# A four-layer decoder trunk: the first norm's squares and row dealt out over later blocks, a load moved to ACT's queue, and halved matmuls in the odd mixer

## The chip, the core and the metric

The kernel runs on one core of a Trainium2 chip. The metric is the time of one execution on the device in microseconds; of several executions the median is given.

## What is computed

The reference is a decoder trunk for 256 positions of 1024 channels: two layers, each with a feed-forward block (FFN), a mixer and a second FFN, all added to the residual with an RMS norm ahead of each. The even layer's mixer is latent attention beside a pooling mixer, the odd one's a gated spatial mixer. Cut to what matters here:

```python
def _rmsnorm(x, g):
    xf = x.astype(jnp.float32)
    y = xf * lax.rsqrt(jnp.mean(xf * xf, axis=-1, keepdims=True) + EPS)
    return (y * g.astype(jnp.float32)).astype(x.dtype)

def _swiglu(x, w_gate, w_up, w_down):
    return (jax.nn.silu(x @ w_gate) * (x @ w_up)) @ w_down
...
        h = h + 0.5 * _swiglu(_rmsnorm(h, ffn_norm[layer, 0]), ffn_w_gate[layer, 0],
                              ffn_w_up[layer, 0], ffn_w_down[layer, 0])
```

All of it is in float32. FFN width is 2816.

## The kernel before

Activations lie transposed, channels on partitions: hT holds eight k tiles of 128 x 256. The order of the work on each engine is the order in which the program is written; nothing is rescheduled.

**Weights** come in chunks of 512 KB, in one list for the whole program (chunks 0 to 43 are the first FFN's gate and up weights, four chunks to a block of 256 hidden channels, so block b uses chunks 4b to 4b+3; a chunk holds two k tiles). A chunk is loaded by SP into one of five `raw` buffers, cast by ACT to a high part `whi` (L170), and DVE takes the difference as the low part `wlo` (L178); I call that DVE step the chunk's split. There are six pairs of high and low. `next_chunk` (L197) hands out a chunk and before that emits the casts and splits of chunks up to three ahead (`LOOK`), fewer for the first chunks (the `min(look, max(1, i - 2))`). The first four chunks, the head, are split in halves or quarters (L182, L183).

**A matmul** of full accuracy is a pair, `mm2` (L215): `wlo` times the high part of x, 256 columns (L217), and `whi` times both parts of x, 512 columns (L218). The two halves of the bank are added when it is evacuated: ACT copies one half (`a`, L325), DVE adds the other (`gu`, L327).

**The FFN** (L355) works through 11 blocks. `gate_up(b)` runs 64 pairs into four PSUM banks, from the pools `acc` and `rot` in turn; `hooks` are called ahead of a given chunk of the block. Then comes the evacuation, then `epilogue(b)`: DVE multiplies by the norm's row, ACT takes silu, DVE multiplies twice, ACT casts, DVE takes the difference (L382 to L388).

**The norm** is applied late. x is only scaled by the gain (`norm_hi` on ACT, `norm_lo` on DVE). The squares are taken by ACT (L274) and summed by POOL (L279). `norm_sum` (L282) sums over partitions on TensorE (L285), DVE adds epsilon (`me`, L288), POOL takes the power (L251) and builds four diagonal matrices (L298), two high and two low. `norm_row` (L301) turns them into a row in PSUM by four matmuls of 128 columns (L305, L307), which ACT copies to `rb` (L310) and DVE halves to `rbh` (L314). In each FFN the sum runs ahead of block 1's first chunk (the bank is one that block 0's evacuation frees) and the row and block 0's epilogue ahead of its third.

**The head of the program** (from L1052): 18 warm-up matmuls on zeros, then loads on SP in turn: par_x0 (gains and the first k tile), the chunk's piece, the next k tile, and so on, then the constants `cst` (identity and masks). For each k tile ACT casts x and the weights and DVE takes the differences; the squares of k tile k-2 follow behind.

**The odd mixer's output** (L1021 on) multiplies `zz`, the gated product, by the output weights, two k tiles to a chunk; `mix_block(3)`, `gate(3)` and `gate_lo(3)` (L1004), which make the last two k tiles of zz, stand behind the first chunk.

## Time and profile before

| | us |
|---|---|
| median of 3 runs | 902.7 (899.63 to 903.33) |
| the profiled execution | 899.92 |
| its span on the core | 898.1 |
| TensorE matmuls busy | 887.7 |
| DVE busy | 651.0 |
| ACT busy | 498.5 |
| POOL busy | 99.7 |

The durations below come from the one profiled execution; its time is the span and 1.8 us around it. A busy TensorE is not one at its peak: matmuls overlap, so what counts is when each starts. Engines are written PE (matmul), PEld (its weight loads), DVE, ACT, POOL and SP; L218 is line 218.

### The profile page before, as it was taken

How to read it: one execution, taken by the hardware profiler on the slowest of the kernel's cores; microseconds unless marked ns; L12 is line 12 of the kernel's file. 1: busy time of each engine (PE TensorE's matmuls, PEld its weight loads, DVE VectorE, ACT ScalarE, POOL GpSimd, SP SyncE). 2: the span in 40 equal slices, each digit the busy share in tenths (PEclk: the TensorE clock that was granted, in tenths of full speed). 3: DMA queues.
4: the chain of work that ended last, by engine and by line, in shares of the span. 5: the costliest groups of instructions: out<-in, count | busy, mean ns of one | idle time of the engine just before them, and what ended most of it. 6: DMA issues, size and time to landing. Idle time of an engine off the chain costs nothing.

```text
span 898.1 us, 13674 instructions
## 1 busy us (share of the span) xinstructions
PE 887.7 (99%) x5204; PEld 783.2 (87%) x5204; DVE 651.0 (72%) x989; ACT 498.5 (56%) x790; POOL 99.7 (11%) x130
## 2 busy tenths in 40 slices
PE   8999999999999999999999999999999999999998
PEld 6888888899898888888888888888888888888887
DVE  7787778667877877785558777756658878777652
ACT  7555554547675655554456555544545666555430
POOL 4200000117524000000130000000120220000000
PEclk9999999999999999999999999999999999999999
DMA  8575556634344555557544555576435556555750
GB/s 291 187 248 195 193 191 194 218 116 161 110 150 141 180 191 196 185 189 241 202 157 149 188 188 188 188 261 190 167 128 168 167 185 202 194 191 189 257 165 24
DMA packets 60306, 164.45 MB, mean 183 GB/s; under 512 B 5457, under 2 KB 7761, under 8 KB 60241
## 3 DMA queue, kind: packets, MB, share of 16 engines
q1 hardware_dynamic: 60240, 163.58, 54.3%
q8 instruction: 41, 0.67, 0.3%
q14 instruction: 25, 0.20, 0.1%
HBM read 162.51 MB, written 1.05 MB: 182 GB/s over the span
## 4 chain that ended last, share of the span: by engine, by line
PE 90%; DVE 5%; POOL 2%; issue 1%; ACT 1%; DMA 1%; SPq 0%; DVEq 0%; ACTq 0%; POOLq 0%
PE acc L218 27%; PE rot L218 27%; PE acc L217 14%; PE rot L217 14%; PE rot L211 1%; PE rot L213 1%; PE rot L212 1%; DVE wlo L178 1%; POOL diag L298 1%; PE acc L212 1%; PE acc L211 1%; PE acc L213 1%; DMA raw<-w_gu 1%; DVE sA L611 0%; DVE z L994 0%
## 5 line engine op out<-in xcount | busy, mean ns | idle before, releaser
L178 DVE TENSOR_TENSOR wlo<-raw,whi 128x1024 fp32r<-128x1024 f32 (+2 forms) x298 | 352.9, 1229 | 71.4 <-ACT whi L170 71.3
L170 ACT CAST whi<-raw 128x1024 fp32r<-128x1024 f32 (+2 forms) x303 | 301.5, 1044 | 101.2 <-PE acc L218 40.5
L218 PE MATMUL acc<-x,whi 128*128 128x512 f32 x768 | 268.2, 392 | 0.0
L218 PE MATMUL rot<-x,whi 128*128 128x512 f32 x704 | 245.6, 392 | 0.0
L217 PE MATMUL acc<-x,wlo 128*128 128x256 f32 x768 | 216.6, 282 | 2.0 <-DVE wlo L183 1.9
L217 PE MATMUL rot<-x,wlo 128*128 128x256 f32 x704 | 197.5, 280 | 0.0
L218 PEld LDWEIGHTS acc<-x,whi 128*128 128x128 f32 x768 | 143.8, 187 | 31.1
L218 PEld LDWEIGHTS rot<-x,whi 128*128 128x128 f32 x704 | 131.7, 187 | 29.0
L217 PEld LDWEIGHTS acc<-x,wlo 128*128 128x128 f32 x768 | 145.4, 189 | 3.7 <-DVE wlo L183 3.2
L217 PEld LDWEIGHTS rot<-x,wlo 128*128 128x128 f32 x704 | 133.1, 189 | 0.0
L218 PE MATMUL rot<-pp,whi 128*128 128x512 f32 x352 | 122.2, 391 | 0.0
L218 PE MATMUL acc<-pp,whi 128*128 128x512 f32 x352 | 122.2, 391 | 0.0
L217 PE MATMUL rot<-pp,wlo 128*128 128x256 f32 x352 | 98.6, 280 | 0.0
L217 PE MATMUL acc<-pp,wlo 128*128 128x256 f32 x352 | 98.6, 280 | 0.0
L218 PEld LDWEIGHTS rot<-pp,whi 128*128 128x128 f32 x352 | 65.8, 187 | 14.4
L218 PEld LDWEIGHTS acc<-pp,whi 128*128 128x128 f32 x352 | 65.8, 187 | 14.4
L217 PEld LDWEIGHTS rot<-pp,wlo 128*128 128x128 f32 x352 | 66.5, 189 | 0.0
L217 PEld LDWEIGHTS acc<-pp,wlo 128*128 128x128 f32 x352 | 66.5, 189 | 0.0
L325 ACT COPY a<-rot 128x256 f32<-128x256 f32 x88 | 29.7, 374 | 52.1 <-PE rot L218 52.1
L325 ACT COPY a<-acc 128x256 f32<-128x256 f32 x88 | 29.7, 374 | 51.2 <-PE acc L218 51.1
L279 POOL TENSOR_TENSOR sqsum<-sq,sq 128x256 f32<-128x256 f32 x6 | 6.0, 1007 | 453.0 <-ACT sq L274 453.0
L383 ACT ACTIVATE gu<-gu 128x512 f32<-128x512 f32 x44 | 27.8, 633 | 50.7 <-DVE gu L382 50.6
(247 smaller groups left out, 937.2 us busy)
## 6 DMA issues: line engine op xcount, KB each, us to landing
raw<-w_gu SPq DMA_DIRECT2D x172, 512.0 KB, 4.7
raw<-w_down SPq DMA_DIRECT2D x88, 512.0 KB, 4.7
raw<-ew_out SPq DMA_DIRECT2D x8, 512.0 KB, 3.6
raw<-ow_v SPq DMA_DIRECT2D x8, 512.0 KB, 3.6
raw<-ow_u SPq DMA_DIRECT2D x8, 512.0 KB, 5.0
raw<-ow_out SPq DMA_DIRECT2D x8, 512.0 KB, 3.7
raw<-ew_p SPq DMA_DIRECT2D x4, 512.0 KB, 4.2
raw<-w_gu SPq DMA_DIRECT2D x7, 256.0 KB, 4.6
```

The lines of the kernel that those rows point to most:

```text
L170: nc.scalar.copy(hi[:, :n], r[:, :n])
L178: eng.tensor_sub(lo[:, :n], r[:, :n], hi[:, :n].bitcast(F32))
L211: nc.tensor.matmul(out, wl, xh, start=start, stop=False, skip_group_check=True)
L212: nc.tensor.matmul(out, wh, xl, start=False, stop=False, skip_group_check=True)
L213: nc.tensor.matmul(out, wh, xh, start=False, stop=stop, skip_group_check=True)
L217: nc.tensor.matmul(bank[:, 0:T], wl, x[:, 1, :], start=start, stop=False, skip_group_check=True)
L218: nc.tensor.matmul(bank, wh, x.rearrange("p s t -> p (s t)"), start=False, stop=stop, skip_group_check=True)
L279: nc.gpsimd.tensor_add(t, s.sum, sq)
L298: nc.gpsimd.tensor_scalar(s.dg[:, i, tb * P : (tb + 1) * P], ident, part[:, tb : tb + 1], None, op0=ALU.mult)
L325: nc.scalar.copy(tmp[:, i, :], bank[:, 0:T])
L383: nc.scalar.activation(t, t, AF.Silu)
```

## The change

- In the head: par_x0 is issued from ACT's queue; the first k tile's cast goes from ACT to DVE; a 19th warm-up matmul; no squares between the casts. `next_chunk` looks three chunks ahead from the start.
- In the first FFN: the squares are taken ahead of block 0's third chunk (k tiles 0 to 3) and fourth (4 to 7), and added by DVE in place of POOL. The constants are loaded ahead of block 0's second chunk, behind the loads of five more chunks. The sum runs ahead of block 1's third chunk. The row runs in two halves, ahead of block 2's second and third chunk, in a bank of its own; block 0's epilogue stands behind the second half, block 1's ahead of block 2's fourth chunk.
- In the other three FFNs the sum stays, the row's first half stays ahead of block 1's third chunk, and its second half and block 0's epilogue go ahead of the fourth.
- In the odd mixer: for the k tile behind `mix_block(3)`, the low-part matmuls of the first two output tiles run in two halves of 128 columns, ahead of both high-part ones.

```diff
-WARM = 18
-SQ_LAG = 2
+WARM = 19
...
-        advance(i + 1 + min(look, max(1, i - 2)), cap)
+        advance(i + 1 + look, cap)
...
-    def norm_sq(s, k):
+    def norm_sq(s, k, eng=nc.gpsimd):
...
-            nc.gpsimd.tensor_add(t, s.sum, sq)
+            eng.tensor_add(t, s.sum, sq)
...
-    def norm_row(s, half=False):
+    def norm_row(s, half=False, bank=None, parts=range(TB)):
+        s.bank = s.bank if bank is None else bank
         bc = s.bank[:, T : 2 * T]
-        for tb in range(TB):
+        for tb in parts:
...
+        if TB - 1 not in parts:
+            return
...
-            gu0 = evacuate(gate_up(0))
-            bank = sets[0]()
+            held = {}
+
+            def late(b):
+                epilogue(b, held.pop(b))
+
+            def row():
+                norm_row(s, bank=sets[1]() if first else None, parts=(0,))
 
             def mid():
-                norm_row(s, half=True)
-                epilogue(0, gu0)
-
-            for b in range(1, NB):
-                gb = gate_up(b, {0: lambda: norm_sum(s, bank), 2: mid} if b == 1 else {})
-                epilogue(b, evacuate(gb))
+                norm_row(s, half=True, parts=(1,))
+                late(0)
+
+            def squares(ks):
+                for k in ks:
+                    norm_sq(s, k, nc.vector)
+
+            if first:
+                hooks = {0: {1: lambda: nc.sync.dma_start(cst_sb, cst), 2: lambda: squares(range(4)),
+                             3: lambda: squares(range(4, KD))},
+                         1: {2: lambda: norm_sum(s, sets[0]())}, 2: {1: row, 2: mid, 3: lambda: late(1)}}
+            else:
+                hooks = {1: {0: lambda: norm_sum(s, sets[0]()), 2: row, 3: mid}}
+            for b in range(NB):
+                held[b] = evacuate(gate_up(b, hooks.get(b, {})))
+                if b > (1 if first else 0):
+                    late(b)
...
+                    n = 2 if j == 1 and k % 2 == 0 else 0
+                    for m in range(n):
+                        ms = slice(m * P, (m + 1) * P)
+                        for tb in range(TB):
+                            ts = slice(tb * P, (tb + 1) * P)
+                            nc.tensor.matmul(banks[m][:, ts], w[1][:, 0, ms], zz[:, k, 1, ts], start=False,
+                                             stop=False, skip_group_check=True)
...
+    nc.scalar.dma_start(par_h[:, 0 : NPAR + T], par_x0)
     preload(AF.Silu)
...
-            if k == 0:
-                nc.sync.dma_start(par_h[:, 0 : NPAR + T], par_x0)
-            else:
+            if k > 0:
                 nc.sync.dma_start(hT[:, k, :], xT[k - 1])
...
-    nc.sync.dma_start(cst_sb, cst)
...
-            norm_hi(s, k)
+            if k == 0:
+                nc.vector.tensor_scalar(s.xh[:, k, :], hT[:, k, :], pcol(s.gname, s.goff), None,
+                                        op0=ALU.mult)
+            else:
+                norm_hi(s, k)
             norm_lo(s, k)
         split(*parts[c], cs, nc.vector)
-        if k not in seen and k >= SQ_LAG:
-            norm_sq(s, k - SQ_LAG)
         seen.add(k)
-    for k in range(KD - SQ_LAG, KD):
-        norm_sq(s, k)
```

How the rows move is shown at three places. First ACT, behind the head, before: the last two casts of the head's casts, the last squares, the casts of chunks 4 and 5 (`raw_219`, `raw_221`), then block 0's evacuation.

```order
L182 CAST whi_145<-raw_133 128x512
L274 ACTIVATE sq_199<-par_h 128x256
L274 ACTIVATE sq_203<-par_h 128x256
L274 ACTIVATE sq_207<-par_h 128x256
L170 CAST whi_277<-raw_219 128x1024
L170 CAST whi_280<-raw_221 128x1024
L325 COPY a_303<-acc_215 128x256
```

The same place in the change; chunks 4 to 7 are `raw_189`, `raw_191`, `raw_193` and `raw_195`.

```order
L181 CAST whi_145<-raw_134 128x512
L169 CAST whi_216<-raw_189 128x1024
L169 CAST whi_219<-raw_191 128x1024
L273 ACTIVATE sq_241<-par_h 128x256
L273 ACTIVATE sq_243<-par_h 128x256
L273 ACTIVATE sq_247<-par_h 128x256
L273 ACTIVATE sq_251<-par_h 128x256
L169 CAST whi_255<-raw_193 128x1024
...
L169 CAST whi_293<-raw_195 128x1024
L327 COPY a_316<-acc_185 128x256
```

Eight squares and the casts of chunks 6 and 7 now stand ahead of block 0's evacuation, and four of the squares ahead of chunk 6's cast.

Second DVE, from `rbh` on in the first FFN, before: block 0's epilogue, the splits of chunks 9 and 10 (`raw_284`, `raw_336`), then block 1's evacuation, all in block 1.

```order
L314 TENSOR_SCALAR rbh_394<-acc_312 128x256
L382 TENSOR_TENSOR gu_302<-gu_302,rb_392 128x512
L384 TENSOR_TENSOR gu_302<-gu_302,rbh_394 128x512
L385 TENSOR_TENSOR gu_302<-gu_302 128x512
L388 TENSOR_TENSOR pp_214<-gu_302,pp_214 128x2x256
L178 TENSOR_TENSOR wlo_367<-raw_284,whi_366 128x1024
L178 TENSOR_TENSOR wlo_403<-raw_336,whi_402 128x1024
L327 TENSOR_TENSOR gu_446<-rot_313,a_447 128x256
```

And in the change, from `rbh` on, in block 2; chunks 13 and 14 are `raw_355` and `raw_393`, and the last row is the first of block 2's evacuation, behind which block 2's epilogue and only then the split of chunk 15 stand.

```order
L316 TENSOR_SCALAR rbh_498<-rot_469 128x256
L384 TENSOR_TENSOR gu_315<-gu_315,rb_496 128x512
L386 TENSOR_TENSOR gu_315<-gu_315,rbh_498 128x512
L387 TENSOR_TENSOR gu_315<-gu_315 128x512
L390 TENSOR_TENSOR pp_184<-gu_315,pp_184 128x2x256
L177 TENSOR_TENSOR wlo_473<-raw_355,whi_472 128x1024
L384 TENSOR_TENSOR gu_433<-gu_433,rb_496 128x512
L386 TENSOR_TENSOR gu_433<-gu_433,rbh_498 128x512
L387 TENSOR_TENSOR gu_433<-gu_433 128x512
L390 TENSOR_TENSOR pp_184<-gu_433,pp_184 128x2x256
L177 TENSOR_TENSOR wlo_507<-raw_393,whi_506 128x1024
L329 TENSOR_TENSOR gu_556<-acc_443,a_557 128x256
```

Two epilogues with a split between them stand behind the row, where before one epilogue and two splits did.

Third DVE in the second FFN, before, from `me` to the epilogue's first row; the splits are of the second FFN's chunks 7 and 8.

```order
L288 TENSOR_SCALAR me_3162<-rot_3155 128x2
L178 TENSOR_TENSOR wlo_3124<-raw_2939,whi_3123 128x1024
L178 TENSOR_TENSOR wlo_3176<-raw_3061,whi_3175 128x1024
L314 TENSOR_SCALAR rbh_3225<-rot_3155 128x256
L382 TENSOR_TENSOR gu_3145<-gu_3145,rb_3223 128x512
```

And in the change.

```order
L287 TENSOR_SCALAR me_3164<-rot_3161 128x2
L177 TENSOR_TENSOR wlo_3126<-raw_2941,whi_3125 128x1024
L177 TENSOR_TENSOR wlo_3178<-raw_3063,whi_3177 128x1024
L177 TENSOR_TENSOR wlo_3200<-raw_3085,whi_3199 128x1024
L316 TENSOR_SCALAR rbh_3249<-rot_3161 128x256
L384 TENSOR_TENSOR gu_3147<-gu_3147,rb_3247 128x512
```

The split of chunk 9 moves from behind the epilogue to ahead of it; one split fewer stands behind.

More of the change, by code (lines that the diff above doesn't have):

```diff
@@ L1028, in odd_mixer @@
                 for k in (2 * j, 2 * j + 1):
-                    for m in range(4):
+                    n = 2 if j == 1 and k % 2 == 0 else 0
[5 more added lines that the diff above has]
+                                             stop=False, skip_group_check=True)
+                    for m in range(n):
+                        ms = slice(m * P, (m + 1) * P)
+                        nc.tensor.matmul(banks[m], w[0][:, 0, ms], zz[:, k].rearrange("p s t -> p (s t)"),
+                                         start=False, stop=False, skip_group_check=True)
+                    for m in range(n, 4):
                         out(k, m, w)
```

## Prediction

> **What bounds the kernel now.** I read the page first, for who is on the chain that ended last; then TensorE's timeline over the first 45 us, looking for starts that come later than the matmul before them allows; then, at each such place, the rows of the engine named there; and last the same places in the later FFNs.
>
> ```profile
> span 898.1 us, 13674 instructions
> ```
>
> TensorE is busy for nearly all of this span, so time is won only where a matmul starts late, and lost only where one is made to. The rows below give start, duration, engine, line and tiles; the bracket is the idle time ahead of the row and what ended it.
>
> ```profile
> 8.01 0.39 PE L217 MATMUL acc<-x,wlo 128*128 128x256 f32 x1 [1.31 <-DVE wlo L183]
> ...
> 19.11 0.39 PE L218 MATMUL acc<-x,whi 128*128 128x512 f32 x1
> 19.93 0.58 PE L285 MATMUL acc<-cmean,sqsum 128*128 128x1 f32 x4 [0.43 <-DVE gu L327]
> 20.37 0.36 PE L217 MATMUL rot<-x,wlo 128*128 128x256 f32 x1
> ...
> 25.78 0.39 PE L218 MATMUL rot<-x,whi 128*128 128x512 f32 x1
> 27.08 0.33 PE L305 MATMUL acc<-diag,ones_r 128*128 128x128 f32 x1 [0.92 <-POOL diag L298]
> ...
> 27.82 0.28 PE L307 MATMUL acc<-diag,ones_r 128*128 128x128 f32 x1
> 27.94 0.33 PE L217 MATMUL rot<-x,wlo 128*128 128x256 f32 x1
> ...
> 33.55 0.28 PE L217 MATMUL acc<-x,wlo 128*128 128x256 f32 x1
> ...
> 36.32 0.28 PE L217 MATMUL acc<-x,wlo 128*128 128x256 f32 x1
> ```
>
> 33.55 and 36.32 are the first matmuls of two chunks that follow each other undisturbed: a chunk costs TensorE 2.77 us, one k tile of it 1.39, and a 512-column matmul (a sixteenth of it and its partner 0.347) about 0.23. With that the waits can be counted. From 8.01 the seven k tiles left of block 0 need 9.71 us and would end at 17.72; the last one ends at 19.11 + 0.23 = 19.34. So block 0 loses 1.62 us. The norm's sum then starts 0.59 us late (19.34 to 19.93). The norm's row stretches from 26.01 (25.78 + 0.23) to 27.94, 1.93 us, most of it waiting for POOL's diagonals. Everything the change can win lies here: 0.4 or so ahead of 8.01, then 1.62, 0.59 and about 1.5.
>
> **A: the first loads.** par_x leaves SP's queue for ACT's, so each SP load moves up by one issue.
>
> ```profile
> 0.72 0.39 SPq L1067 DMA_DIRECT2D par_h<-par_x  x1
> 1.17 0.90 SPq L1072 DMA_DIRECT2D raw<-w_gu  x2
> ...
> 2.00:3.00 1.00, 1.00 (x7) 0.69 (x6) 0.00 (x0) 0.20 (x2) 0.09 (x1) 1.00 0.76 252
> 14.00:15.00 1.00, 0.74 (x5) 0.69 (x5) 1.00 (x2) 1.00 (x3) 0.74 (x1) 1.00 1.04 388
> ...
> cst_sb<-cst SPq DMA_DIRECT2D x1, 298.0 KB, 5.3
> ...
> par_h<-par_x SPq DMA_DIRECT2D x1, 160.5 KB, 2.3
> ```
>
> The issue that goes is 0.45 us long (0.72 to 1.17). In the window rows the last two columns are the DMA engines' share and GB/s: 0.76 of them are already busy at 2 us, so not all of the 0.45 need arrive. I take 0.40 for the wait at 8.01, with 0.2 and 0.45 as ends. The Trainium skill ("Trainium Kernel Development and Optimization", Key Constraints) speaks against more: DMAs of all issuing queues share the same 16 engines, and a second queue only saves issue time. Without that rule one could hope for the whole transfer of par_x, 160.5 KB at 252 GB/s, 0.64 us; with it A ends at 0.45. The 19th warm-up matmul and the first k tile's cast on DVE cost nothing: the first k tile waits there for the second one's weights in either kernel (the 1.31 us at 8.01). The constants' load, moved behind five weight loads, sends chunk 4 and those behind it 298 KB / 388 GB/s = 0.77 us earlier on top. A = -0.40.
>
> **B: block 0 without the squares.** Here the squares leave ACT's line between the casts, and POOL's sums go.
>
> ```profile
> 7.26 0.69 DVE L183 TENSOR_TENSOR wlo<-raw,whi 128x512 fp32r<-128x512 f32 x1 [1.42 <-ACT whi L182]
> 7.87 0.48 DVE L269 SCALAR_TENSOR_TENSOR x<-par_h,x 128x256 fp32r<-128x256 f32 x1
> ...
> 11.67 1.99 POOL L279 TENSOR_TENSOR sqsum<-sqsum,sq 128x256 f32<-128x256 f32 x2 [0.37 <-ACT sq L274]
> ...
> 12.11 0.96 DVE L269 SCALAR_TENSOR_TENSOR x<-par_h,x 128x256 fp32r<-128x256 f32 x1
> ```
>
> The same L269 takes 0.48 us at 7.87 and 0.96 at 12.11, while a POOL sum runs. With POOL idle a k tile costs DVE 0.69 + 0.48 = 1.17 us at most, under TensorE's 1.39, so the 1.62 us of waits go; I leave 0.13 of them for a later tile's weights that land late. B = -1.49; at worst, if landings set the pace of every other tile, half of it comes (-0.8), at best -1.62.
>
> **C: the squares' new place.** They stand on ACT behind chunk 5's cast, the first three adds on DVE ahead of chunk 5's split.
>
> ```profile
> 14.79 1.03 ACT L274 ACTIVATE sq<-par_h 128x256 f32<-128x256 f32 x3
> ...
> 17.40 1.05 ACT L170 CAST whi<-raw 128x1024 fp32r<-128x1024 f32 x1 [0.25 <-DMA raw<-w_gu]
> ```
>
> Chunk 5 landed just ahead of 17.40; with A and the constants gone it lands near 16.2. From there: cast 1.05, four squares about 1.34 (three take 1.03) and some 0.3 more, since the fourth needs the first's buffer back, an add of about 0.48 (an L269 of the same width) and chunk 5's split, 1.22 (E has its rows): done near 20.6. Block 0 now ends near 17.45, so TensorE wants chunk 5 at 17.45 + 2.77 = 20.2 and waits 0.3. Two chunks on, the norm's sum needs a bank that block 0's evacuation frees; that evacuation stands on ACT behind four more squares and two casts, and I allow 0.2. So 0.5 in place of 0.59: C = -0.1, between -0.59 (nothing late) and +1.1 (the constants' 0.77 and A not arriving at chunk 5).
>
> **D: the norm's row in block 2.** It now comes 8.3 us (three chunks) behind its sum rather than two chunks, and in two halves of two matmuls.
>
> ```profile
> 20.70 0.15 DVE L288 TENSOR_SCALAR me<-acc 128x2 f32<-128x2 f32 x1
> 24.28 2.17 POOL L298 TENSOR_SCALAR diag<-cst_sb,r_hi 128x128 fp32r<-128x128 f32 x2
> 26.43 1.18 POOL L298 TENSOR_SCALAR diag<-cst_sb,r_lo 128x128 fp32r<-128x128 f32 x2
> ...
> 281.93 0.15 DVE L288 TENSOR_SCALAR me<-rot 128x2 f32<-128x2 f32 x1
> 285.81 1.19 POOL L298 TENSOR_SCALAR diag<-cst_sb,r_lo 128x128 fp32r<-128x128 f32 x2
> ...
> 287.18 0.22 PE L305 MATMUL rot<-diag,ones_r 128*128 128x128 f32 x1
> ...
> 287.46 0.28 PE L307 MATMUL rot<-diag,ones_r 128*128 128x128 f32 x1
> ```
>
> From "me" to the end of the third diagonal, which the first half needs, POOL took 6.33 us here (to 27.03) and 4.5 in the second FFN (to 286.4), where DVE was idle at the time. "me" itself now stands on DVE behind four adds, three splits and an evacuation that follow chunk 5's split at 20.6 (4 x 0.4 + 3 x 1.135 + 1.33 = 6.3): near 26.9. The first half is due at 17.45 + 0.5 + 0.44 (the sum's rows, 19.93 to 20.37) + 5 x 2.77 = 32.25. That leaves 5.35 us; DVE runs splits for the first part of the chain and an evacuation later, so I take the middle of the two chains, 5.4, and a wait of 0.05 to 0.1. The Trainium skill ("SBUF — State Buffer", SBUF: two separate sides) has the shared port as an exclusive lock that a DVE operation takes against POOL when it has two SBUF inputs; the evacuation's adds read one operand from PSUM, which by that rule leaves POOL free there. By the rule D has no wait; by the chain from 20.70 it has 0.98. The rows themselves cost 0.39 in the second FFN (287.18 to 287.57), and in halves about 0.17 twice. So 1.93 becomes 0.44: D = -1.49, between -1.59 and -0.6.
>
> **E: two epilogues behind one row.** This is the new bill. Block 0's and block 1's epilogues both stand behind the row's second half, in block 2.
>
> ```profile
> 28.88 0.68 DVE L382 TENSOR_TENSOR gu<-gu,rb 128x512 f32<-128x512 f32 x1
> ...
> 32.26 2.35 DVE L178 TENSOR_TENSOR wlo<-raw,whi 128x1024 fp32r<-128x1024 f32 x2
> 34.53 1.41 DVE L327 TENSOR_TENSOR gu<-rot,a 128x256 f32<-128x256 f32 x4
> 35.86 0.69 DVE L382 TENSOR_TENSOR gu<-gu,rb 128x512 f32<-128x512 f32 x1
> ...
> 39.24 4.63 DVE L178 TENSOR_TENSOR wlo<-raw,whi 128x1024 fp32r<-128x1024 f32 x4
> ```
>
> An epilogue holds DVE for 3.38 us (28.88 to 32.26, 35.86 to 39.24), a split 1.135 (two from 32.26 to 34.53), an evacuation 1.33 (34.53 to 35.86). The last row matmul started at 27.82, the epilogue at 28.88: 1.06 later. In the changed order DVE then has epilogue, split of 13, epilogue, split of 14, evacuation, epilogue, split of 15: 3 x 3.38 + 2 x 1.135 + 1.33 + 1.22 (what is left of 4.63 for the first of four) = 14.96, so chunk 15 is split 16.0 us behind the row. TensorE gets to it after 0.11 and five chunks, 13.97 us. It waits about 2.05 us, once; chunk 16, a split further on, has 2.77 us more. E = +2.05, 1.6 to 2.3; it falls to nothing only if DVE is not the engine that ends last there, which no row suggests.
>
> **F: the same in the second to fourth FFN.** The epilogue moves from block 1's third chunk to its fourth.
>
> ```profile
> 298.87 3.49 DVE L178 TENSOR_TENSOR wlo<-raw,whi 128x1024 fp32r<-128x1024 f32 x3
> ...
> 301.50 0.28 PE L217 MATMUL rot<-x,wlo 128*128 128x256 f32 x1
> ...
> 739.37 3.49 DVE L178 TENSOR_TENSOR wlo<-raw,whi 128x1024 fp32r<-128x1024 f32 x3
> ...
> 741.77 0.28 PE L217 MATMUL rot<-x,wlo 128*128 128x256 f32 x1
> ```
>
> In the second FFN the first of the splits at 298.87 ends at 300.09, 1.41 us ahead of its matmul at 301.50. The row comes 2.77 later, and one split less (1.135) stands behind it: 1.41 - 2.77 + 1.135 = -0.23, with some 0.06 from DVE to TensorE a wait of 0.29. The third FFN is alike; in the fourth, where the split ends at 740.59, it is 1.18 - 1.64 - 0.06 = -0.52. Sum 1.10, less 0.05 a row for the halves: F = +0.95, between 0 and 1.5 (three waits like the fourth's). In these FFNs the row never waited in the first place (287.18 follows on the matmul before it), so nothing is won against it.
>
> **G: the odd mixer.** Two matmuls more of 128 columns, some 0.11 each like those of the row.
>
> ```profile
> 695.82 0.19 PEld L218 LDWEIGHTS rot<-zz,whi 128*128 128x128 f32 x1 [0.52 <-DVE zz L1004]
> ```
>
> Two chunks later TensorE waits 0.52 us for DVE's last zz, whose time DVE's own line sets; the 0.2 goes into that wait. G = 0, +0.2 without that cover.
>
> **The sum**: -0.40 - 1.49 - 0.10 - 1.49 + 2.05 + 0.95 = -0.5 us. The profiled execution took 899.92 us, 1.8 more than its span and 2.8 less than the median of the runs, so it would become 899.4; the median, 902.7, becomes 902.2. That is no change that can be measured: about 0.5%, 4.5 us, is what a measurement of this kernel can tell.
>
> **Rivals.** *The gain stays.* E and F don't come, because the splits behind the epilogues are not late. For it speaks that TensorE shows no such wait in any FFN before; against it that every term of E is a measured row and that DVE works in order. With E gone and F down to its -0.15 the sum is -3.6 and the time 899.1. *Slower by POOL's chain.* The first half of the row in block 2 waits for the third diagonal. It decides once the chain from "me" takes over 5.95 us (the 5.35 that are there, the 0.1 counted above and the 0.5 of the forecast): with the 6.33 of before it costs 0.9 more and the time is 903.1; with three diagonals at the 1.08 of the first pair (3.58 us to 24.28, and 3.24) the chain is 6.8, the wait 1.5 and the time 903.6. For it: "me" now falls among DVE's splits, as at 20.70. Against it: the evacuation in between. *The change does less than it says.* The squares leave block 0, but its weights come no earlier and DVE doesn't follow: A -0.2, B -0.8, C 0 and the rest as forecast, +0.5, 903.2.
>
> **How the numbers follow.** The forecast, a gain or loss of under two us with both new waits there: 0.57. The gain stays: 0.18. Slower by POOL's chain: 0.12. Does less: 0.08. Beyond 4.5 us to either side, which no sum here reaches (the best ends are -0.45 - 1.62 - 0.59 - 1.59 - 0.15 = -4.4 with E and F gone): 0.05 in all. The range runs from 898.6, just past the first rival, to 904.4, the second rival's 903.6 and most of C's upper end. Faster by over 0.5% 0.04, slower 0.03, no change 0.93.
>
> **What the profile would show.** A: the second k tile starts near 7.6 rather than 8.01. B: block 0's last matmul ends near 17.5. C: a wait of some tenths ahead of block 1's second chunk, and another at the sum. D: next to no idle ahead of either row half. E: about 2 us of idle ahead of block 3's fourth chunk, ended by DVE's split. F: 0.3 to 0.5 ahead of block 2's fourth chunk in each later FFN. The prediction is wrong if E's idle is missing while the order is as shown, or if block 0 ends past 18.5.

## The result, and the profile after

The changed kernel takes 909.2 us (median of 8 runs, 904.4 to 911.6) against 902.8 us (8 runs beside them, 899.6 to 903.3): a ratio of 1.0079, 95% interval 1.0059 to 1.0099. That is slower by 0.8%, outside the range of 898.6 to 904.4 and on the side that was given a chance of 0.03. The profiled execution of the changed kernel took 910.33 us with a span of 908.5; the one of before 899.92 and 898.1. So there are 10.4 us to find between these two executions; between the medians it is 6.4 us, because both kernels' times lie in two groups (before 899.6 to 900.3 and 902.7 to 903.3, after 904.4 to 905.0 and 908.1 to 911.6), and the profiled executions are from the lower group of the one and the upper of the other.

The places that the prediction named come first. These are TensorE's rows in the changed kernel (start, duration, line, tiles, idle time ahead and what ended it); L216 and L217 are the matmuls that were L217 and L218 before, L284 the norm's sum, L305 and L307 the row.

```profile
8.37 0.39 PE L216 MATMUL acc<-x,wlo 128*128 128x256 f32 x1 [0.86 <-DVE wlo L182]
...
18.20 0.28 PE L216 MATMUL rot<-x,wlo 128*128 128x256 f32 x1
...
23.78 0.40 PE L217 MATMUL rot<-x,whi 128*128 128x512 f32 x1
24.57 0.58 PE L284 MATMUL acc<-cmean,sqsum 128*128 128x1 f32 x4 [0.40 <-DVE gu L329]
...
33.57 0.22 PE L305 MATMUL rot<-diag,ones_r 128*128 128x128 f32 x1
33.63 0.27 PE L307 MATMUL rot<-diag,ones_r 128*128 128x128 f32 x1
...
50.73 0.39 PE L217 MATMUL rot<-x,whi 128*128 128x512 f32 x1
52.79 0.39 PE L216 MATMUL rot<-x,wlo 128*128 128x256 f32 x1 [1.67 <-DVE wlo L177]
...
304.05 0.39 PE L217 MATMUL rot<-x,whi 128*128 128x512 f32 x1
304.56 0.39 PE L216 MATMUL rot<-x,wlo 128*128 128x256 f32 x1
...
748.41 0.39 PE L217 MATMUL rot<-x,whi 128*128 128x512 f32 x1
749.13 0.39 PE L216 MATMUL rot<-x,wlo 128*128 128x256 f32 x1 [0.33 <-DVE wlo L177]
```

With a 512-column matmul counted at 0.23 us, as in the prediction: block 0 has lost its waits and ends at 18.20 instead of 19.34; the sum waits 0.56 us; the row's first half waits for nothing; the wait ahead of chunk 15 is there, 52.79 - 50.73 - 0.23 = 1.83 us; and those ahead of chunk 11 of the later FFNs are there, 0.28 us in the second and 0.49 in the fourth (0.27 in the third). Nearly every wait is where it was expected, and all of them together do not make 10 us. So the next view is the stretches where nothing waits. Here are four windows of 60 us, one in each FFN, of before; the second field behind the window is TensorE's busy time with the number of matmuls, and the field ahead of the last two is its granted clock.

```profile
60.00:120.00 60.00, 60.00 (x349) 52.91 (x348) 48.36 (x65) 35.33 (x54) 2.07 (x1) 1.00 0.56 188
375.00:435.00 60.00, 60.00 (x348) 52.91 (x347) 41.67 (x53) 31.68 (x44) 2.25 (x2) 1.00 0.63 211
565.00:625.00 60.00, 60.00 (x347) 52.89 (x347) 39.34 (x50) 30.76 (x42) 2.24 (x2) 1.00 0.64 213
820.00:880.00 60.00, 60.00 (x348) 52.91 (x347) 38.22 (x48) 27.59 (x34) 0.00 (x0) 1.00 0.57 191
```

And the same windows of the changed kernel.

```profile
60.00:120.00 60.00, 60.00 (x341) 52.02 (x340) 47.92 (x65) 36.09 (x55) 1.32 (x1) 1.00 0.57 196
375.00:435.00 60.00, 60.00 (x347) 52.90 (x347) 42.83 (x56) 32.23 (x44) 1.79 (x2) 1.00 0.62 207
565.00:625.00 60.00, 60.00 (x342) 52.00 (x341) 41.02 (x52) 30.84 (x42) 2.20 (x2) 1.00 0.65 210
820.00:880.00 60.00, 60.00 (x342) 52.05 (x341) 41.46 (x54) 29.43 (x39) 0.00 (x0) 1.00 0.61 206
```

TensorE is busy for all 60 us in both, at a granted clock of 1.00 in both. But it gets through 348 matmuls in the one case and 341 or 342 in the other: in the first, third and fourth FFN the stream runs 2% slower although nothing is late. The start times, to the nanosecond, show what differs. From one 512-column matmul to the 256-column one behind it, it is 230 ns each time in the *short cadence*, and in the *long cadence* a cycle of about 233, 236 and 241 ns. A stretch keeps one of them for hundreds of matmuls. A chunk of eight pairs (so that a block has 32 pairs, not the 64 of the kernel's description, which counts matmuls) takes 2.773 us in the first FFN of before (55.73 to 194.40, 50 chunks) and 2.827 in the changed kernel (55.71 to 197.05).

The starts of the same places in both traces give the whole account (an FFN's end is the start of the first matmul behind it):

| place | before | after | after - before |
|---|---|---|---|
| second k tile of block 0 | 8.01 | 8.37 | +0.36 |
| first chunk of block 2 | 33.55 | 30.75 | -2.80 |
| first chunk of block 4 | 55.73 | 55.71 | -0.02 |
| first FFN's end | 194.40 | 197.05 | +2.65 |
| second FFN, block 3 | 304.27 | 307.45 | +3.18 |
| third FFN, chunk 7 | 474.57 | 477.94 | +3.37 |
| third FFN's end | 638.19 | 644.93 | +6.74 |
| fourth FFN, chunk 2 | 715.60 | 721.95 | +6.35 |
| fourth FFN, chunk 13 | 747.32 | 754.89 | +7.57 |
| the end | 898.1 | 908.5 | +10.4 |

Summed over the steps from one 512-column start to the next, 8.7 of the 10.4 us are cadence (3.1 in the first FFN, 3.0 in the third, 3.0 in the fourth, 0.4 won back in the odd mixer), and 1.7 are the waits gone and come, with the restarts behind them. In the first FFN the long cadence begins at the wait of 0.12 us ahead of chunk 5 (20.74 to 21.09 us), and the 1.83 us ahead of chunk 15 do not end it; in the third and fourth it begins, for the rest of the FFN, at the wait ahead of chunk 11.

### The profile page after: what moved, and what is told of

Its sections match the earlier page's. It is cut to its first block, busy times and chain, and to the rows that moved or that the text cites. A ratio compares the mean times of both kernels' runs of the same rounds, so it can differ in the third digit from the quotient of the medians.

```text
span 908.5 us, 13677 instructions
## 1 busy us (share of the span) xinstructions
PE 898.1 (99%) x5207; PEld 784.8 (86%) x5207; DVE 650.4 (72%) x997; ACT 498.8 (55%) x789; POOL 95.1 (10%) x123
## 3 DMA queue, kind: packets, MB, share of 16 engines
HBM read 162.51 MB, written 1.05 MB: 180 GB/s over the span
## 4 chain that ended last, share of the span: by engine, by line
PE 82%; DVE 9%; ACT 3%; issue 2%; DMA 2%; POOL 2%; SPq 0%; POOLq 0%; DVEq 0%; ACTq 0%
PE acc L217 24%; PE rot L217 24%; PE acc L216 12%; PE rot L216 12%; DVE wlo L177 3%; DMA raw<-w_gu 2%; PE rot L210 1%; PE rot L212 1%; PE rot L211 1%; PE acc L211 1%; PE acc L210 1%; DVE par_h L333 1%; PE acc L212 1%; DVE gu L329 1%; ACT whi L169 1%
## 5 line engine op out<-in xcount | busy, mean ns | idle before, releaser
L217 PE MATMUL acc<-x,whi 128*128 128x512 f32 x768 | 271.5, 396 | 0.0
L217 PE MATMUL rot<-x,whi 128*128 128x512 f32 x704 | 248.4, 396 | 0.0
L216 PE MATMUL acc<-x,wlo 128*128 128x256 f32 x768 | 217.2, 283 | 1.0 <-DVE wlo L182 0.9
L216 PE MATMUL rot<-x,wlo 128*128 128x256 f32 x704 | 198.2, 282 | 2.1 <-DVE wlo L177 2.0
L217 PEld LDWEIGHTS acc<-x,whi 128*128 128x128 f32 x768 | 144.6, 188 | 33.6
L217 PEld LDWEIGHTS rot<-x,whi 128*128 128x128 f32 x704 | 132.2, 188 | 31.2
L216 PEld LDWEIGHTS acc<-x,wlo 128*128 128x128 f32 x768 | 145.6, 190 | 2.2 <-DVE wlo L182 1.4
L216 PEld LDWEIGHTS rot<-x,wlo 128*128 128x128 f32 x704 | 133.0, 189 | 3.3 <-DVE wlo L177 3.3
L217 PE MATMUL acc<-pp,whi 128*128 128x512 f32 x352 | 124.0, 397 | 0.0
L217 PE MATMUL rot<-pp,whi 128*128 128x512 f32 x352 | 124.0, 397 | 0.0
L216 PE MATMUL acc<-pp,wlo 128*128 128x256 f32 x352 | 98.8, 281 | 0.0
L216 PE MATMUL rot<-pp,wlo 128*128 128x256 f32 x352 | 98.8, 281 | 0.0
L217 PEld LDWEIGHTS rot<-pp,whi 128*128 128x128 f32 x352 | 66.1, 188 | 16.0
L217 PEld LDWEIGHTS acc<-pp,whi 128*128 128x128 f32 x352 | 66.1, 188 | 16.0
L216 PEld LDWEIGHTS rot<-pp,wlo 128*128 128x128 f32 x352 | 66.5, 189 | 0.0
L216 PEld LDWEIGHTS acc<-pp,wlo 128*128 128x128 f32 x352 | 66.5, 189 | 0.0
L329 DVE TENSOR_TENSOR gu<-acc,a 128x256 f32<-128x256 f32 x88 | 31.3, 419 | 30.0 <-ACT a L327 29.9
```

Source lines behind the costliest of these rows:

```text
L216: nc.tensor.matmul(bank[:, 0:T], wl, x[:, 1, :], start=start, stop=False, skip_group_check=True)
L217: nc.tensor.matmul(bank, wh, x.rearrange("p s t -> p (s t)"), start=False, stop=stop, skip_group_check=True)
L329: nc.vector.tensor_add(out[:, i, :], bank[:, T:], tmp[:, i, :])
```

## The experiments

The theory at this point: whenever another engine stops TensorE's stream, the stream starts again in one or the other cadence and keeps it, so each new wait costs its own length and, at times, 2% of all that follows. Three rivals: the halves of the row make the long cadence, not the wait; the changed head or another placement in memory makes it; or waits are all there is and the cadence is a bystander. Behind each run's edit stands what was expected of it.

The outcomes in one table. The last column counts the matmuls that TensorE did in the four windows above in the profiled execution; 347 to 349 is the short cadence, 341 or 342 the long one. Ratios are to the kernel before, run on the same chip; the changed kernel was timed only for the result, so distances to its 909.2 us are between different sessions.

| run | median us (range, runs) | ratio (95%) | matmuls in 60 us, FFN 1, 2, 3, 4 |
|---|---|---|---|
| e1_whole_row | 900.7 (898.5 to 903.4, 12) | 0.9988 (0.9973 to 1.0002) | 347, 348, 348, 347 |
| e2_halves_no_wait | 902.8 (899.6 to 906.0, 12) | 0.9999 (0.9984 to 1.0014) | 348, 348, 348, 342 |
| e3_halves_on_before | 909.5 (907.8 to 911.6, 6) | 1.0076 (1.0059 to 1.0092) | 348, 341, 348, 341 |
| e4_wait_elsewhere | 900.2 (899.5 to 903.1, 12) | 0.9992 (0.9977 to 1.0007) | 341, 349, 349, 347 |
| e4b_wait_whole_row | 905.3 (902.1 to 908.3, 6) | 1.0060 (1.0039 to 1.0081) | 348, 348, 348, 348 |
| e11_wait_second_look | 906.5 (1 run; before 903.0) | | 347, 341, 348, 342 |
| e5_spread_first_ffn | 900.2 (897.1 to 901.7, 11) | 0.9995 (0.9986 to 1.0005) | 341, 348, 348, 349 |
| e6_after_reset | 904.1 (903.5 to 905.1, 5) | 1.0047 (1.0035 to 1.0059) | 348, 348, 349, 348 |
| e10_two_matmuls | 906.0 (903.0 to 908.9, 6) | 1.0067 (1.0049 to 1.0084) | 341, 348, 348, 348 |
| e7_whole_row_no_wait | 897.5 (896.8 to 898.3, 8) | 0.9973 (0.9963 to 0.9983) | 348, 348, 348, 348 |
| e8_norm_sum_later | 896.8 (896.4 to 899.1, 5) | 0.9970 (0.9958 to 0.9982) | 348, 349, 348, 348 |
| e9_without_odd_halves | 898.1 (896.9 to 899.0, 11) | 0.9978 (0.9969 to 0.9986) | 348, 348, 349, 347 |

The kernel before has two groups of times itself: on the chip of e1 to e4 12 of its 29 runs took 899.3 to 900.4 us and 17 took 902.6 to 903.6; on the two chips of e4b to e10 all 37 took 899.3 to 901.0. In its second to fourth FFN a row that waits for nothing follows on the norm's sum; in the first the row itself is a stop, of 0.9 us.

### Term F undone

```
+            def whole():
+                norm_row(s, half=True)
+                late(0)
...
-                hooks = {1: {0: lambda: norm_sum(s, sets[0]()), 2: row, 3: mid}}
+                hooks = {1: {0: lambda: norm_sum(s, sets[0]()), 2: whole}}
```

> The kernel after, with the row of the second, third and fourth FFN in one piece at the place it had before (in block 1 ahead of the third chunk, with block 0's epilogue), so that term F is undone and all else stays. Theory (a stop of TensorE draws its cadence anew: the start-to-start of the 512-column matmuls is then either 230 ns, or 232 to 241 ns up to the next stop, about 3.1 us an FFN): the three waits of 0.28, 0.27 and 0.49 us go, FFN 2 to 4 run at 230 ns throughout, and the times stand at about 900.2 or 903.3 us, by how FFN 1's waits fall. Rival 1 (it is the row in halves that makes the slow cadence, not the wait): the same times. Rival 2 (the changed head or another placement in memory makes it): the long cadence stays in FFN 3 and 4, and the times stay at 903.5 to 911 us.

Measured: 900.7 us, 8.5 under the changed kernel, and the short cadence in the windows of FFN 2 to 4. The three waits that went are 1.05 us together. The second rival (head or placement) expected 903.5 to 911 and falls as far as the head goes, which is still the changed one. The wait of 1.82 us ahead of chunk 15 is still there as well (49.90 in this trace), and in this execution the first FFN came out of it in the short cadence.

### The halves without the wait

```
-                norm_row(s, bank=sets[1]() if first else None, parts=(0,))
+                norm_row(s, bank=sets[1](), parts=(0,))
...
-                hooks = {1: {0: lambda: norm_sum(s, sets[0]()), 2: row, 3: mid}}
+                hooks = {1: {0: lambda: norm_sum(s, sets[0]())}, 2: {1: row, 2: mid},
+                         3: {1: lambda: late(1), 3: lambda: late(2)}, 4: {2: lambda: late(3)}}
...
-                if b > (1 if first else 0):
+                if b > (1 if first else 3):
```

> The kernel after, with the halves of the row in FFN 2 to 4 put into block 2 (ahead of its second and third chunk), and the epilogues of blocks 0 to 3 spread over blocks 2 to 4, so that no split is late; FFN 1 as after. Theory (a wait redraws the cadence): no wait ended by a split in FFN 2 to 4, their 512-column matmuls at 230 ns, time 900.2 or 903.3 us as with the whole row. Rival 1 (the halves make the slow cadence): the stretches behind the halves run at about 236 ns in two or three of these FFNs, 904 to 911 us. Rival 2 (head or placement): 903.5 to 911 us too, with the slow stretches beginning elsewhere than at the halves.

Measured: 899.6 to 906.0 us. No split is late in FFN 2 to 4, and 902.8 lies 6.4 under the changed kernel, so the wait carries most of the loss. But the theory's 900.2 or 903.3 was missed upward, by runs near 906. The trace shows why, here with the last two of the four windows.

```profile
565.00:625.00 60.00, 60.00 (x348) 52.91 (x347) 39.23 (x50) 30.32 (x42) 2.23 (x2) 1.00 0.64 214
820.00:880.00 60.00, 60.00 (x342) 52.02 (x341) 38.55 (x48) 26.80 (x34) 0.00 (x0) 1.00 0.59 200
```

And the second half of the fourth FFN's row in TensorE's timeline, with the matmuls around it.

```profile
735.81 0.40 PE L217 MATMUL rot<-x,whi 128*128 128x512 f32 x1
736.05 0.22 PE L305 MATMUL acc<-diag,ones_r 128*128 128x128 f32 x1
736.10 0.27 PE L307 MATMUL acc<-diag,ones_r 128*128 128x128 f32 x1
736.22 0.33 PE L216 MATMUL rot<-x,wlo 128*128 128x256 f32 x1
```

The fourth FFN takes the long cadence at the norm's sum (721 us, a wait of 0.21, of which some 0.13 stands at every sum) and keeps it through both halves to the end. The half stands there without any wait and changes nothing. In e4_wait_elsewhere the fourth FFN leaves its sum in the long cadence as well, and the whole row ends it: 236 ns ahead of the row at 730 us, 230 behind it. So the theory was short of a part: the whole row sets the cadence, and the halves do so only at times. In the third FFN of this trace the first half does, at 480.07 us: 236.8 ns ahead of it, 230 behind. What the halves do not do is begin the long cadence: over all traces, a half or pair of short matmuls that waited for nothing and had the short cadence ahead of it had it behind it in 11 of 11 cases. That speaks against the first rival.

### Term F alone, on the kernel before

Here `norm_row` takes `parts` as in the change, and all else is the kernel before.

```
...
+            hooks = {1: {0: lambda: norm_sum(s, sets[0]())}}
+            if first:
+                hooks[1][2] = whole
+            else:
+                hooks[1].update({2: row, 3: mid})
...
```

> The kernel before, with term F alone: in FFN 2 to 4 the row in halves ahead of the third and fourth chunk of block 1, and block 0's epilogue behind the second half. Theory (a wait redraws the cadence): waits of 0.3 to 0.5 us ahead of the last chunk of block 2 in FFN 2 to 4 as in the kernel after (about +1 us), and a new draw of the cadence behind each, 0 to 3.1 us an FFN: runs spread from 901 to 911 us, median about 906. Rival 1 (halves): the same or steadier, near 910. Rival 2 (head or placement): only the waits' own 1 us, 900.9 or 903.9 us.

Measured: 907.8 to 911.6 us, all of the loss with none of the new head. Second rival refuted a second time; by it this run had to be at 900.9 or 903.9. In the trace the second FFN turns long at the row's first half, which waits 0.16 us for GpSimd's diagonals, and the fourth is long from ahead of its norm's sum.

### A wait far from the row

```
...
+            hooks = {1: {0: lambda: norm_sum(s, sets[0]()), 2: mid}}
+            if not first:
+                hooks[6] = {3: lambda: late(5)}
+            for b in range(NB):
+                held[b] = evacuate(gate_up(b, hooks.get(b, {})))
+                if b > 0 and (first or b != 5):
+                    late(b)
```

> The kernel before, whole row and all, with one thing changed in FFN 2 to 4: block 5's epilogue is held until ahead of the last chunk of block 6, so that two epilogues stand behind one another on VectorE ahead of a split, as in term F but far from the row. Theory (a wait redraws the cadence): a wait of 0.2 to 0.5 us ended by a split at the end of block 7's third chunk in each of the three FFNs (about +1 us), and from there to the FFN's end, somewhat over half of it, 230 ns or the long cadence by chance (0 to 1.8 us each): 900.9 to 909 us, runs spread, median about 903.5 to 905. Rival 1 (halves): the waits alone, 900.9 or 903.9 us, all of FFN 2 to 4 at 230 ns. Rival 2 (head or placement): the same as rival 1.

Measured: no wait came about, so this run tells nothing on waits. VectorE takes the moved epilogue out of time in which it stood idle; ahead of the next block's evacuation 1.76 us are still left:

```profile
351.23 1.42 DVE L327 TENSOR_TENSOR gu<-rot,a 128x256 f32<-128x256 f32 x4 [1.76 <-ACT a L325]
```

Its trace is of use for the first FFN: behind the row's wait at 27 us it runs in the long cadence to the end, which comes at 197.38 us instead of 194.40 in before's trace. That 3.0 us is the distance between before's two groups of times.

The next form of it makes the wait for certain:

```
...
                 held[b] = evacuate(gate_up(b, hooks.get(b, {})))
+                if b == 6 and not first:
+                    late(5)
...
```

> The kernel before, whole row and all, with one thing changed in FFN 2 to 4: block 5's epilogue stands on VectorE directly behind block 6's evacuation, ahead of block 6's own, so that the next split comes about 3.35 us later (the epilogue's length) where 2.77 us are to spare. Theory (a wait redraws the cadence, with the row whole too): a wait of about 0.6 us ahead of the last chunk of block 7 (or the third) in each of the three FFNs, +1.7 us in sum, and from there, somewhat over half of the FFN, 230 ns or the long cadence by chance (0 to 1.8 us each): 901.6 to 910 us, spread, median about 905. Rival 1 (only the halves of the row make the slow cadence): 901.6 or 904.7 us, FFN 2 to 4 at 230 ns behind the wait too. Rival 2 (only the missing reset by a whole row right behind the norm's sum): the same as rival 1.

> The same kernel as e4b_wait_whole_row, once more for its trace: there the times went from 902.1 to 908.3 us, and the profiled execution was the fastest of them, at 230 ns behind all three waits. Theory (each wait draws the cadence): an execution of 904 us or more has the 512-column matmuls at about 236 ns from the wait at the end of block 7's third chunk to the FFN's end, in as many of the three FFNs as it lies steps of about 2 us above 902.1, and at 230 ns between the whole row and the wait in all of them. Rival (the spread has another cause, such as the head or the mixers): an execution as slow has 230 ns behind all three waits.

Measured: waits of 0.65 us in all three FFNs, and times from 902.1 to 908.3 us, which is what the theory asks for and the first rival (901.6 or 904.7) doesn't give. The profiled execution was the fastest, in the short cadence behind all three. The second execution traced (e11) took 906.5 us, 4.4 above it, and has the long cadence behind two of the three waits. Its rows at the wait in the second FFN:

```profile
356.88 0.39 PE L218 MATMUL acc<-x,whi 128*128 128x512 f32 x1
357.78 0.39 PE L217 MATMUL acc<-x,wlo 128*128 128x256 f32 x1 [0.50 <-DVE wlo L178]
```

And its four windows:

```profile
60.00:120.00 60.00, 60.00 (x347) 52.88 (x346) 48.37 (x65) 35.45 (x54) 1.91 (x1) 1.00 0.56 189
375.00:435.00 60.00, 60.00 (x341) 52.02 (x341) 41.04 (x53) 32.16 (x44) 2.19 (x2) 1.00 0.60 203
565.00:625.00 60.00, 60.00 (x348) 52.91 (x347) 40.67 (x52) 30.59 (x42) 2.25 (x2) 1.00 0.65 217
820.00:880.00 60.00, 60.00 (x342) 52.06 (x341) 40.16 (x50) 29.00 (x36) 0.00 (x0) 1.00 0.61 202
```

The first FFN runs short, and so does each of the others from its row to its wait (230.0 ns over 199 matmuls in each). The same program, the same waits, and another cadence behind two of them: the cadence is drawn anew at the wait, with the row whole and the head as it was. A placement in memory can't be the cause of that either, since the program is the same.

### Four short matmuls, and two

At the start of `gate_up` in the changed kernel; e10_two_matmuls has `range(2)`.

```
+                if b == 4:
+                    for i in range(4):
+                        nc.tensor.matmul(banks[0][:, 0:P], ones_r, s.dg[:, i % 2, 0:P], start=True, stop=True,
+                                         skip_group_check=True)
```

> The kernel after with all its waits, and four extra matmuls of 128 columns at the start of block 4 in each FFN, into a bank that the block's first matmul then overwrites (work that the reference does not ask for). They cost about 0.1 us each by the halves of the row, so 1.4 us in all four FFNs. Theory (the loss is TensorE's cadence, drawn at the waits; a run of four short matmuls without a wait sets it to 230 ns): from block 4 on all four FFNs run at 230 ns, and the time falls from 909 to about 901.2 + 1.4 + up to 1 for the stretches ahead of block 4, 902.5 to 904 us, in a narrow group. Rival 1 (the slow cadence is a lasting state of the kernel's placement, or of the changed head): 910 us, 1.4 over the kernel after. Rival 2 (short matmuls draw anew, as a wait does): a spread from 902.5 to 912 us.

> As e6_after_reset (904.1 us), with two extra matmuls at the start of block 4 of each FFN instead of four. Theory (a row of four short matmuls sets the cadence to 230 ns, a half row of two does not: it leaves the cadence as it is or draws anew): stretches at about 236 ns behind block 4 in some FFNs, runs spread from 903.4 to 911 us, median over 905. Rival (any short matmul without a wait sets it): a narrow group at 903.4 to 904 us, the price of two matmuls (0.2 us an FFN) lower than e6 at most.

Measured with four: 903.5 to 905.1 us, 5 us under the changed kernel by adding work. All four FFNs were long ahead of the extra matmuls and short behind them. These are they, in the first FFN:

```profile
55.90 0.56 PE L364 MATMUL acc<-diag,ones_r 128*128 128x128 f32 x4
```

And the windows behind:

```profile
60.00:120.00 60.00, 60.00 (x348) 52.91 (x348) 48.28 (x65) 36.22 (x55) 1.45 (x1) 1.00 0.59 202
375.00:435.00 60.00, 60.00 (x348) 52.91 (x348) 41.53 (x53) 32.67 (x45) 2.25 (x2) 1.00 0.61 205
565.00:625.00 60.00, 60.00 (x349) 52.91 (x348) 40.36 (x52) 30.11 (x41) 2.24 (x2) 1.00 0.65 219
820.00:880.00 60.00, 60.00 (x348) 52.91 (x347) 40.36 (x50) 29.02 (x37) 0.00 (x0) 1.00 0.60 202
```

Both rivals expected 910 or a spread up to 912. With two, the group spreads from 903.0 to 908.9 us, and the first FFN goes on in the long cadence behind them:

```profile
55.19 0.33 PE L364 MATMUL acc<-diag,ones_r 128*128 128x128 f32 x2
```

```profile
60.00:120.00 60.00, 60.00 (x341) 52.08 (x340) 46.75 (x65) 35.56 (x54) 2.19 (x1) 1.00 0.57 199
```

So four such matmuls in a row set the short cadence and two do not do so reliably (in this execution the third and the fourth FFN turned short at them, the first did not).

### Without the waits

On e1_whole_row, in the first FFN; e7_whole_row_no_wait has `2: {2: whole}` in the second line, in a bank of `sets[1]`.

```
-                         1: {2: lambda: norm_sum(s, sets[0]())}, 2: {1: row, 2: mid, 3: lambda: late(1)}}
+                         1: {2: lambda: norm_sum(s, sets[0]())}, 2: {1: row, 2: mid},
+                         3: {1: lambda: late(1), 3: lambda: late(2)}, 4: {2: lambda: late(3)}}
...
-                if b > (1 if first else 0):
+                if b > (3 if first else 0):
```

> The kernel after, with the row of FFN 2 to 4 whole as before (as in the run e1_whole_row), and in FFN 1 the epilogues of blocks 1 to 3 spread over blocks 3 and 4 (ahead of the second and fourth chunk of block 3 and the third of block 4) instead of closing up behind the row's halves, which stay. Term E: the wait of 1.82 us ahead of chunk 15 goes. Theory (a stop draws the cadence, four short matmuls of a whole row without a wait set it to 230 ns, halves of two leave it as it is or draw anew): FFN 1 is then left with whatever cadence came out of the wait at the norm's sum (23.4 to 24.6 us), which was the long one in all three kernels with this head that have been seen, and nothing stops TensorE again up to the FFN's end: spans 1.8 us lower than with the wait where FFN 1 runs fast (896.7 to 898 us), and about 1.2 us higher where it runs slow (899.7 to 901 us). Rival (the wait itself is all, the cadence does not hang on it): 898.8 us median, 1.8 under the 900.7 of e1_whole_row, whatever the cadence.

> As the run beside it (FFN 1's epilogues spread, the row of FFN 2 to 4 whole), and in FFN 1 the row whole too, ahead of the third chunk of block 2, where both halves had stood without a wait. Theory (a whole row of four short matmuls that does not wait sets the cadence to 230 ns): all four FFNs at 230 ns from their row on, one group of times, 896.7 to 898 us, no run near 901. Rival (short matmuls do nothing to the cadence, only waits do): two groups of times, 897 and 900 us, as in the run with the halves.

Measured with the halves: two groups, 897.1 to 898.3 us (4 runs) and 900.1 to 901.7 (7 runs). Term E's wait is gone and the median of e1_whole_row is hardly moved (900.7 to 900.2, on two chips), which fits the theory: nothing behind the long cadence ends it any more (236.7 ns from 36 to 194 us in the profiled execution). The profiled execution, 900.1 us, is of the upper group:

```profile
60.00:120.00 60.00, 60.00 (x341) 52.09 (x340) 47.88 (x65) 35.21 (x54) 1.53 (x1) 1.00 0.59 198
```

With the row whole at a place where it doesn't wait: one group, 896.8 to 898.3 us, faster than the kernel before in all its runs (ratio 0.9973, 0.9963 to 0.9983). The rival without a role for the short matmuls expected two groups. In e7's own trace the first FFN ran short ahead of its row already; a row that ends the long cadence there stands in e8's, below. Then, each by itself on e7, the norm's sum a chunk later (e8_norm_sum_later) and the odd mixer's halves taken back (e9_without_odd_halves):

```
-                         1: {2: lambda: norm_sum(s, sets[0]())}, 2: {2: whole},
+                         1: {3: lambda: norm_sum(s, sets[0]())}, 2: {2: whole},
...
-                    n = 2 if j == 1 and k % 2 == 0 else 0
+                    n = 0
```

> As e7_whole_row_no_wait (897.5 us median), with FFN 1's norm sum one chunk later (ahead of block 1's fourth chunk instead of its third). There TensorE waited 0.60 us for VectorE's sums of squares in e7's profile; a chunk later they are done. GpSimd's chain behind it has from about 27 us to the row at 36.9 us, more than it takes. Theory (each wait in the head counts in full, and the whole row behind it sets the cadence anyway): 896.9 us, a narrow group. Rival (GpSimd's chain or the splits behind the sums are late next, ahead of the row or of chunk 7): 897.5 us or over, with a new wait of 0.6 us or more there.

> As e7_whole_row_no_wait, with the odd mixer's small-term matmuls in one piece again as before (part G undone). Theory: the wait behind the odd mixer's last mixing grows from about 0.1 to about 0.5 us (+0.4), and the stretch from there to the norm's sum of FFN 4 (some 70 pairs) may fall into the long cadence, 0 to 0.45 us: 897.9 to 898.4 us. Rival (the halves are hidden, as the prediction's term G of nothing had it): 897.5 us.

Measured: 896.8 us with the later sum, 0.7 less, as expected, though the intervals of the two ratios overlap; the row at 36.25 us follows on the matmul ahead of it and sets the cadence from 236 to 230 ns. It is the best version found, 0.30% under the kernel before (0.9970, 0.9958 to 0.9982). Without the odd halves the median is 898.1 us, 0.6 more than e7, again within the intervals, and the mechanism expected for it is not seen: from the odd mixer's first matmul to the fourth FFN's third chunk the traces take either about 77.0 or 77.4 us, and both values occur with the halves (77.0 in the changed kernel, 77.4 in e8) and without (77.1 in e4b, 77.4 in e9). The halves are hidden; what varies there is the cadence.

## Why the prediction was wrong

**The step that failed** is the sum. It took from the starts at 33.55 and 36.32 that "a chunk costs TensorE 2.77 us" and carried that through the span, so that a wait costs its own length and no more. The same chunk takes 2.83 us in the other cadence, and the two kinds of edit that the sum priced at some tenths, a wait ahead of chunk 11 and a row cut in halves, decide which one runs for the next 100 us and more. 8.7 of the 10.4 us came from there. Nothing in the prediction's own rows said so, but the trace of before did: its 512-column matmuls run long from 270 to 281 us and from 696 to 721 us, up to the norm's sum each time, and short behind it. The prediction went by late starts only, and a stream that is slow throughout has none.

**A was wrong in sign.** The second k tile started at 8.37 us, not 7.6. The load of its weights was issued 0.48 us earlier (at 2.10 instead of 2.58) and landed no earlier (the cast that waits for it began at 6.97 instead of 6.61), while par_x, now beside SP's loads instead of ahead of them, took 3.0 us to land where it had taken 2.3:

```profile
par_h<-par_x ACTq DMA_DIRECT2D x1, 160.5 KB, 3.0
```

How far this tile's start varies by itself shows over the traces: from 7.26 to 8.41 us in the five with the old head, from 7.74 to 9.34 in the nine with the new one, of which these are the ends (in e5_spread_first_ffn and e9_without_odd_halves).

```profile
7.74 0.39 PE L216 MATMUL acc<-x,wlo 128*128 128x256 f32 x1 [0.57 <-DVE wlo L182]
```

```profile
9.34 0.38 PE L216 MATMUL acc<-x,wlo 128*128 128x256 f32 x1 [2.46 <-DVE wlo L182]
```

So A is nothing, within several tenths, rather than -0.40. The rule that the prediction drew from the Trainium skill ("Trainium Kernel Development and Optimization", Key Constraints), that queues share the DMA engines and a second one saves issue time alone, was not applied far enough: the trace agrees that the loads share, and here not even the issue time arrived.

**B was right**: block 0 ends at 18.20, 9.83 us behind its second k tile where before needed 11.33, so -1.50 against -1.49. **C** came to about +0.1 instead of -0.1: 0.12 us ahead of chunk 5 and 0.56 at the sum against 0.59. **D was right**: neither half waits, -1.55 against -1.49. By the page "SBUF — State Buffer" (SBUF: two separate sides) of the Trainium skill a VectorE operation holds the port it shares with GpSimd when it has two SBUF inputs, so that the evacuation, with one operand in PSUM, leaves GpSimd free. The trace agrees: two diagonals in 1.20 us beside the evacuation, two in 2.97 beside splits.

```profile
30.29 1.49 DVE L329 TENSOR_TENSOR gu<-rot,a 128x256 f32<-128x256 f32 x4 [0.26 <-ACT a L327]
31.69 2.38 DVE L177 TENSOR_TENSOR wlo<-raw,whi 128x1024 fp32r<-128x1024 f32 x2
...
30.32 1.20 POOL L297 TENSOR_SCALAR diag<-cst_sb,r_hi 128x128 fp32r<-128x128 f32 x2
31.49 2.97 POOL L297 TENSOR_SCALAR diag<-cst_sb,r_lo 128x128 fp32r<-128x128 f32 x2
```

**E was right**, 1.83 against 2.05. **F** had the splits' waits right to a few hundredths (0.28, 0.27, 0.49 against 0.29, 0.29, 0.52) and the sum too small: with the small waits of the row's first half for GpSimd (0.16, 0.05, 0.22 us), the sum's wait in the fourth FFN (0.33, of which every sum has some 0.13) and the restarts, the three FFNs lose about 2.3 us without any cadence, not 0.95. The waits for GpSimd come from the split of chunk 9, which now stands ahead of the epilogue: GpSimd's `r_lo`, which fell behind two splits in before, falls beside the third in the changed kernel and takes 1.07 us instead of 0.19 (0.20 in e1_whole_row, which has two again). Here it is in the second FFN, first before, then after.

```profile
282.00 2.35 DVE L178 TENSOR_TENSOR wlo<-raw,whi 128x1024 fp32r<-128x1024 f32 x2
284.47 0.19 POOL L294 TENSOR_TENSOR r_lo<-r,r_hi 128x2 f32<-128x2 f32 x1
```

```profile
284.50 3.49 DVE L177 TENSOR_TENSOR wlo<-raw,whi 128x1024 fp32r<-128x1024 f32 x3
286.98 1.07 POOL L293 TENSOR_TENSOR r_lo<-r,r_hi 128x2 f32<-128x2 f32 x1
```

The prediction had the row of these FFNs wait for nothing. **G was right**: nothing.

The terms without the cadence thus come to +1.7 us where -0.5 was forecast, which alone would have put the median at 904.4, the very end of the range. By the medians, 6.4 us apart, that leaves 4.7 for the cadence; this is an estimate, since it takes the waits from the two traced executions. Of the rivals none held the cause; "slower by POOL's chain" had the right side for a reason that did not happen.

**What stays open**: why TensorE has two cadences, and what in a restart picks one. The granted clock is 1.00 in both. Over all fourteen traces, 20 waits of 0.25 us or more behind block 0 were ended by a split; 9 were followed by the short cadence and 11 by the long one. Nor does a change need a late engine: where nothing held up the norm's sum (it started 0.12 to 0.14 us behind the 0.23 of the 512-column matmul ahead), the cadence went from short to long at it in 5 of 12 cases, the third FFN of the changed kernel among them, and from long to short in 17 of 24.

## What to carry to other kernels

Count a saturated engine's work per unit of time in windows where nothing waits, before and after: a stream that is busy all the time can still be 2% slower, and no list of waits shows it. A small wait in the middle of a long matmul stream can cost the rest of the stream, so hand work that lies in the shadow of one block to the next in such a way that no split comes late, and mind the spread of the times, since steps of equal size speak of a state that is drawn again and again. When a kernel holds a short sequence that happens to restore the good state, as the whole row did here, cutting it up has a price that its own duration doesn't tell.

## What the runs showed of the hardware

- In these streams (pairs of a 256- and a 512-column matmul, each with its own weights) TensorE has two steady cadences, 230 ns from a 512-column start to the next, or about 233, 236 and 241 in turn, at a granted clock of 1.00. The long one costs about 3.0 us an FFN. A third, 231 and 233 in turn, is seen in the odd mixer's first 15 pairs in every trace and for 85 pairs around the fourth FFN's start in e6_after_reset.
- In the FFNs, four matmuls of 128 columns on end, with no idle time ahead, were followed by the short cadence in 34 of 34 cases, 13 of which had been long. Two on end ended the long one in 3 of 23 cases and began it in none of 11. Behind block 0, a long one that nothing disturbed never ended by itself.
- A wait can change either into the other: 0.12 us began a long one (chunk 5 of the changed kernel), 0.16 us another (the row's first half in the second FFN of e3_halves_on_before), and 1.82 us turned a long one short twice (e1_whole_row, e2_halves_no_wait).
- In the head, a load beside another queue's loads lands later: par_x took 2.2 to 2.3 us in the five traces where it went ahead of SP's other loads and 3.0 to 3.2 in the nine where it went beside them. The landings behind it vary by over a microsecond from one execution to the next (6.3 to 7.9 us for the same half chunk with the new head).
- A GpSimd operation of 0.19 us took 1.07 when it fell beside VectorE's splits, and ended when they did (288.05 and 287.99 us, second FFN of the changed kernel).
